# Three weight tiles through the contraction side by side at the start, and the bias table's copy moved into the pairs

## The chip, the cores and the metric

The kernel runs on one core of a Trainium2 chip. TensorE (PE) multiplies, with its weight loads shown on a row of their own (PEld); VectorE (DVE), ScalarE (ACT) and GpSimd (POOL) do the element-wise work; SyncE (SP) issues most transfers. The metric is the device time of one execution in microseconds (us); the time before is the median of three runs. One execution was also taken with the hardware profiler; all rows and stages below are of that execution, counted from its first instruction.

## The reference

One layer of a streaming encoder, 512 tokens of 1024 features, all float32. Two SwiGLU feed-forward parts (FFN 1 and FFN 2, hidden width 2816) stand around a mixer with a gated linear recurrence and a sliding-window attention. What matters here is FFN 1 and the bias of the attention:

```python
h = x + 0.5 * post1(SwiGLU_1(pre1(x)))
# swiglu(x, w1, w3, w2) = (silu(x @ w1) * (x @ w3)) @ w2
# rms_norm(x, g)        = x * rsqrt(mean(x * x) + 1e-6) * g
u = pre_mix(h)
# ... q, k, v, recurrent branch A, attention branch B with a shared relative-position bias ...
bias = band_rel_bias(rel_bias)     # (heads, 64, 192), from a (32 buckets, 16 heads) table
sc = sc + bias
h = h + post_mix(merged @ w_o)
y = h + 0.5 * post2(SwiGLU_2(pre2(h)))
```

## The kernel before, in words

Every float32 operand of a product is split in two float32r parts: hi is ACT's rounded copy, lo is DVE's difference (`split2`, L173). A product is then three matmuls, hi by hi, lo by hi, hi by lo (`mm_feat`, L185 to L187). A weight tile is 128 x 1024: one output block of 128 features by the whole contraction of 1024, which is eight blocks `k` of 128. One tile against x^T of all 512 tokens is a *unit*: 24 matmuls of 512 columns into one PSUM bank.

`order` lists the weight tiles in the order of their use. `dma_to(n)` issues loads up to the n-th on SP (L129), `split_to(n)` splits them (L140, L141), and `get` takes the next tile and keeps two splits and three loads ahead. SBUF tiles come from one pool of 38 equal slots (`NSLOT`, L1071). A new tile that takes a slot waits until the slot's last user has finished, and that wait is put on the first instruction that touches the new tile. Each engine runs its instructions in the order in which the code emits them. `later(n, fn)` defers emission by n `point()`s, one of which comes at each half unit.

The start (L546 to L601): nine matmuls on zeros (L561) run first. SP issues the table `vec`, the first w1 tile in two parts, x^T in eight row blocks of 256 KB (L554), then the next weight tiles and x. For each `k`, ACT and DVE scale the block of x^T by the norm's gain and split it into `uT` (L583, L584). Then come the units w1 0, w3 0, w1 1 (L585), one after the other over all eight blocks, then the squares of x and the inverse root mean square (`rstd_of`, L589 to L593), the unit w3 1, and a product `r` that spreads the inverse root over the partitions (L598). `Rb` is its copy, and `silu_mul` applies it to the banks.

The bias table: POOL loads a one-hot table and `rel_bias` (L625, L626). One product makes the 16 x 383 row table (L628), DVE evicts it into `erow` (L630), and POOL issues a transfer that writes it 128 times for each head into DRAM as `bias_scr`, 3064 KB (L633). The attention reads it much later (`bias_load`, L890).

FFN 1 goes on with units up to hidden block 5 (`swiglu_units`, `NC1`), then with `Pairs` (L433): hidden blocks two by two, each pair of w1 blocks a *job*, each pair of w3 blocks the next one, sixteen jobs counted from 0. A job makes seven half-size products in place of eight from sums of weight quarters and of x quarters. `prep(m, 0)` lets POOL form the sums S12 and S34 of job m (L470 to L473), `prep(m, 1)` to `prep(m, 4)` split tiles and sums. `run` (L486) emits job n: the products a11 and s1, each copied by ACT (q1 at L501, q5 at L503), the last product a22 of the job before (`last`), `prep(n+1, 1)`, s2, `prep(n+1, 2)`, a12, s4, `prep(n+1, 3)`, s3 with ACT's copy `v` (L520), `prep(n+1, 4)`, `prep(n+2, 0)` and the loads of job n+3. Before the first job four splits write further x sums into `uT` (L690 to L693).

Of the kernel before, what the change touches and what calls it, by code (L numbers as in the profile page):

```python
# [10 lines left out]
F32 = mybir.dt.float32  # L11
F32R = mybir.dt.float32r
AF = mybir.ActivationFunctionType
ALU = mybir.AluOpType

P = 128
SEQ = 512
D = 1024
KT = D // P
# [3 lines left out]
N_HEADS = 16  # L23
# [5 lines left out]
NREL = 383  # L29
# [22 lines left out]
def hybrid_layer(ctx: ExitStack, tc: tile.TileContext, a: dict, out: bass.AP):  # L52
    nc = tc.nc
    act, dve, pool, pe, sp = nc.scalar, nc.vector, nc.gpsimd, nc.tensor, nc.sync
# [8 lines left out]
    def slot(shape, dt=F32, name="s"):  # L63
        uid[0] += 1
        return sb.tile(shape, dt, tag="slot", name=f"{name}_{uid[0]}")

    def bank(name="ps"):
        uid[0] += 1
        return pp.tile([P, 512], F32, tag="ps", name=f"{name}_{uid[0]}")
# [5 lines left out]
    def f32(ap):  # L75
        return ap.bitcast(F32)
# [10 lines left out]
    uT = cp.tile([P, 2, KT, SEQ], F32R, name="uT")  # L87


    order = []  # L90
# [31 lines left out]
    st = {"dma": 0, "split": 0, "get": 0}  # L122
    raws, pairs = {}, {}

    def dma_to(n):
        while st["dma"] < min(n, len(order)):
            nm, i = order[st["dma"]]
            r = slot([P, D], name=f"raw_{nm}{i}")
            sp.dma_start(out=r, in_=a[nm][i * P : (i + 1) * P, :])  # L129
            raws[st["dma"]] = r  # L130
            st["dma"] += 1

    def split_to(n):
        while st["split"] < min(n, len(order)) and st["split"] not in paired:
            k = st["split"]
            dma_to(k + 1)
            r = raws.pop(k)
            hi = slot([P, D], F32R, name="whi")
            lo = slot([P, D], F32R, name="wlo")
            act.activation(hi, r, AF.Copy)  # L140
            dve.tensor_tensor(out=lo, in0=r, in1=f32(hi), op=ALU.subtract)  # L141
            pairs[k] = (hi, lo)
            st["split"] += 1
# [29 lines left out]
    def split2(hi, lo, src):  # L173

        act.activation(hi, src, AF.Copy)  # L175
        dve.tensor_tensor(out=lo, in0=src, in1=f32(hi), op=ALU.subtract)  # L176
# [14 lines left out]
    def unit(nm, i, **kw):  # L191
        w = get(nm, i)
        ps = bank("f")
        mm_feat(ps, w, **kw)
        return ps
# [225 lines left out]
    def mm_s(wa, x, ps, more=False):  # L421

        wh, wl = wa
        for k in range(4):
            s = slice(k * P, (k + 1) * P)
            xh, xl = x(0, k), x(1, k)
            first = k == 0 and not more
            pe.matmul(ps, wh[:, s], xh, start=first, stop=False, skip_group_check=True)  # L428
            pe.matmul(ps, wl[:, s], xh, start=False, stop=False, skip_group_check=True)  # L429
            pe.matmul(ps, wh[:, s], xl, start=False, stop=k == 3, skip_group_check=True)  # L430
        point()

    class Pairs:  # L433
# [49 lines left out]
                W["a22"] = t[:, 0, :], t[:, 1, :]  # L483
                del W["r"], W["s"]

        def run(self, tail):  # L486
            X = self.X
            assert st["get"] == st["split"] == self.k0, (st, self.k0)
            st["get"] = st["split"] = self.k0 + 2 * len(self.jobs)
            last = lambda: None  # L490
            for n, (nm, f) in enumerate(self.jobs):
                W = self.w.pop(n)
                first = nm == self.na
                tmp = slot([P, 4, 256], name="ct")
                q1, q5, u, v = (tmp[:, i, :] for i in range(4))
                c = slot([P, 2, SEQ], name="cc")
                if first:
                    self.c1[f] = c
                bu, bx, bc = (bank("c")[:, :256] for _ in range(3))
                mm_s(W["a11"], X["b11"], bu)  # L500
                act.activation(q1, bu, AF.Copy)  # L501
                mm_s(W["s1"], X["t1"], bx)
                act.activation(q5, bx, AF.Copy)  # L503
                last()
                self.prep(n + 1, 1)
                mm_s(W["s2"], X["t2"], bu, True)
                del W["s1"], W["s2"]
                act.activation(u, bu, AF.Copy)
                if n == len(self.jobs) - 1:
                    tail()  # L510
                self.prep(n + 1, 2)
                mm_s(W["a12"], X["b21"], bc)
                del W["a11"], W["a12"]
                dve.tensor_tensor(out=c[:, 0, :256], in0=bc, in1=q1, op=ALU.add)
                mm_s(W["s4"], X["b22"], bx, True)
                dve.tensor_tensor(out=c[:, 0, 256:], in0=bx, in1=u, op=ALU.add)
                self.prep(n + 1, 3)
                mm_s(W["s3"], X["t3"], bu, True)
                del W["s3"], W["s4"]
                act.activation(v, bu, AF.Copy)  # L520
                dve.tensor_tensor(out=c[:, 1, 256:], in0=v, in1=q5, op=ALU.add)
                if first:
                    act.activation(c[:, 0, :], c[:, 0, :], AF.Silu)
                    act.activation(c[:, 1, 256:], c[:, 1, 256:], AF.Silu)
                else:
                    c1 = self.c1[f]
                    dve.tensor_tensor(out=c1[:, 0, :], in0=c1[:, 0, :], in1=c[:, 0, :], op=ALU.mult)
                    dve.tensor_tensor(out=c1[:, 1, 256:], in0=c1[:, 1, 256:], in1=c[:, 1, 256:], op=ALU.mult)
                self.prep(n + 1, 4)
                self.prep(n + 2, 0)  # L530
                self.raws(n + 3)

                def last(W=W, bu=bu, c=c, f=f, first=first):
                    mm_s(W.pop("a22"), X["t4"], bu, True)
                    if first:
                        act.activation(c[:, 1, :256], bu, AF.Silu)
                    else:
                        c1 = self.c1.pop(f)
                        dve.tensor_tensor(out=c1[:, 1, :256], in0=bu, in1=c1[:, 1, :256], op=ALU.mult)
                        self.hid.f += [c1[:, 0, :], c1[:, 1, :]]  # L540

            last()

    raw = slot([P, D], name="raw_first")  # L546
    hi, lo = slot([P, D], F32R, name="whi"), slot([P, D], F32R, name="wlo")
    pairs[0] = (hi, lo)
    st["dma"] = st["split"] = 1
    parts = (slice(0, 2 * P), slice(2 * P, D))  # L550
    xts = [slot([P, 2, SEQ], name="xt") for _ in range(KT // 2)]

    def load_x(k):
        sp.dma_start(out=xts[k // 2][:, k % 2, :], in_=a["xT"][k * P : (k + 1) * P, :])  # L554


    warm = slot([P, 512], F32R, name="warm")
# [2 lines left out]
    for _ in range(WARM):  # L560
        pe.matmul(psw, warm[:, :P], warm, start=True, stop=True)  # L561

    sp.dma_start(out=vec, in_=a["vec"])
    sp.dma_start(out=raw[:, parts[0]], in_=a["w1a"][0:P, parts[0]])
    load_x(0)
    load_x(1)
    sp.dma_start(out=raw[:, parts[1]], in_=a["w1a"][0:P, parts[1]])
    for k in range(2, KT):
        load_x(k)
    dma_to(4)  # L570
    for t in range(NT):
        sp.dma_start(out=h_all[:, t, :], in_=a["x"][t * P : (t + 1) * P, :])
    make_identity(nc, ident)
    ones = slot([P, P], name="ones")
    pool.memset(ones, 1.0)
    for k in range(KT):
        if k in (0, 2):
            c = parts[k // 2]
            act.activation(hi[:, c], raw[:, c], AF.Copy)
            dve.tensor_tensor(out=lo[:, c], in0=raw[:, c], in1=f32(hi[:, c]), op=ALU.subtract)  # L580
        g = vec[:, V_G1 + k : V_G1 + k + 1]
        xk = xts[k // 2][:, k % 2, :]
        act.activation(uT[:, 0, k, :], xk, AF.Copy, scale=g)  # L583
        dve.scalar_tensor_tensor(out=uT[:, 1, k, :], in0=xk, scalar=g, in1=f32(uT[:, 0, k, :]), op0=ALU.mult, op1=ALU.subtract)  # L584
    ps = [unit("w1a", 0), unit("w3a", 0), unit("w1a", 1)]  # L585
    s4 = small(NT, "s4")
    for t in range(NT):
        junk = slot([P, D], name="junk")
# [32 lines left out]
        dve.tensor_scalar(out=cneg, in0=z[3], scalar1=-8.0, scalar2=None, op0=ALU.mult)  # L621


    oh = slot([N_BUCKETS, NREL + 1 + N_HEADS], name="oh")
    pool.dma_start(out=oh[:, : NREL + 1], in_=a["onehot"])  # L625
    pool.dma_start(out=oh[:, NREL + 1 :], in_=a["rel_bias"])  # L626
    pse = bank("e")
    pe.matmul(pse[:N_HEADS, : NREL + 1], oh[:, NREL + 1 :], oh[:, : NREL + 1], start=True, stop=True)  # L628
    erow = slot([N_HEADS, NREL + 1], name="erow")
    dve.tensor_copy(erow, pse[:N_HEADS, : NREL + 1])  # L630
    scr = tc.dram_tile([N_HEADS, P, NREL], F32, name="bias_scr")
    ev = erow[:, :NREL]
    pool.dma_start(out=scr, in_=bass.AP(tensor=ev.tensor, offset=ev.offset, ap=[ev.ap[0], [0, P], ev.ap[1]]))  # L633

    def swiglu_units(na, nb, f0, f1, hid, R=None):
        for f in range(f0, f1):
# [46 lines left out]
    pairs_a = Pairs("w1a", "w3a", NC1, X1, hid)  # L683
# [16 lines left out]
        hid.to(2)  # L700
        split_to(st["split"] + 1)

    pairs_a.run(w2_ahead)
    X1 = pairs_a = None
    later(10, softplus)
    bs = tok_gemm("w2a", hid, FT, RF, "ffn1_post_g", 0.5, "mix_pre_g", [("xr", i) for i in range(4)], hid.to)
    hid = None
# [101 lines left out]
    for i in range(8):  # L809
        ps = unit("wg", i)  # L810
# [320 lines left out]
```

## Time and profile before

| | |
|---|---|
| median of three runs | 1161.41 us (1159.35 to 1165.38) |
| the profiled execution | 1161.51 us, span 1159.7 us |
| mean granted TensorE clock | 0.994 |
| PE busy / DVE / ACT / POOL | 98% / 67% / 50% / 32% of the span |
| transfers | 120.73 MB, mean 104 GB/s |

A row of the timeline gives start, duration, engine, line, operation, what it writes from what, and in brackets the idle time of the engine before it with what ended that. A row of the chain of waits gives start, length and what the chain passed through. A row of a stage gives its length, then busy time and number of instructions for PE, PEld, DVE, ACT and POOL, then the granted clock, the share of the transfer engines and GB/s. A matmul's busy time overlaps the next one's; the distance of two starts is its real cost.

### The profile page before, as it was taken

Reading aid. Unit: us, or ns where it says so; the run is one execution under the profiler, and the core shown is the slowest. Engines: PE = TensorE matmul, PEld = TensorE weight load, DVE = VectorE, ACT = ScalarE, POOL = GpSimd, SP = SyncE. Lnnn points to the kernel's source line nnn. Section 1 sums busy time; section 2 is a strip of 40 time slices with the busy share of each in tenths; the row PEclk is TensorE's granted clock in tenths of the full one; section 3 lists DMA queues with packets and bytes.
Section 4 is the critical chain, followed back from the end, with each engine's and each line's share of the span. In section 5 each row is a group of like instructions: output and inputs, shape, how many; then the busy total and the mean of one; then the engine's idle time right before and its main releaser. Section 6 shows DMA issues by size and latency. Waiting matters only on the chain.

```text
span 1159.7 us, 17087 instructions
## 1 busy us (share of the span) xinstructions
PE 1139.1 (98%) x6691; PEld 1011.0 (87%) x6691; DVE 776.8 (67%) x1179; ACT 578.9 (50%) x1023; POOL 365.6 (32%) x271
## 2 busy tenths in 40 slices
PE   8989999999999999999999999999999999999997
PEld 6879999988888888878888788888899999998886
DVE  4997788876437742697667863667868688885313
ACT  6345555564324446864646565355645555564211
POOL 0246777600001001101556550000646667700000
PEclk9999999999999999999999999999999999999999
DMA  9663332254314122224132224342133223254101
GB/s 363 104 135 92 110 110 92 84 207 163 109 37 128 55 62 66 74 73 156 63 91 73 73 73 127 109 146 73 37 110 109 83 100 110 92 176 170 54 19 54
DMA packets 34496, 120.73 MB, mean 104 GB/s; under 512 B 4144, under 2 KB 4272, under 8 KB 34416
## 3 DMA queue, kind: packets, MB, share of 16 engines
q1 hardware_dynamic: 31968, 111.22, 28.3%
q0 software_dynamic: 2448, 8.43, 3.8%
q8 instruction: 52, 0.85, 0.3%
q14 instruction: 28, 0.23, 0.1%
HBM read 114.40 MB, written 5.23 MB: 103 GB/s over the span
## 4 chain that ended last, share of the span: by engine, by line
PE 81%; DVE 8%; ACT 5%; DMA 4%; issue 1%; POOL 1%; SPq 0%; DVEq 0%; POOLq 0%; ACTq 0%
PE c L428 10%; PE c L429 10%; PE c L430 10%; PE f L187 8%; PE f L186 8%; PE f L185 8%; PE acc L205 8%; PE acc L203 8%; PE acc L204 8%; DMA bias_scr<-erow 3%; DVE wlo L141 1%; PE pt L945 1%; POOL P L929 1%; ACT whi L140 1%; DVE ig_e L771 1%
## 5 line engine op out<-in xcount | busy, mean ns | idle before, releaser
L185 PE MATMUL f<-uT,whi 128*128 128x512 f32 (+1 forms) x560 | 206.3, 368 | 1.4 <-ACT uT L583 0.9
L186 PE MATMUL f<-uT,wlo 128*128 128x512 f32 (+1 forms) x560 | 205.1, 366 | 2.4 <-DVE wlo L141 2.4
L187 PE MATMUL f<-uT,whi 128*128 128x512 f32 (+1 forms) x560 | 204.9, 366 | 0.7 <-DVE uT L283 0.4
L203 PE MATMUL acc<-whi,hT 128*128 128x512 f32 x352 | 137.1, 390 | 0.0
L204 PE MATMUL acc<-wlo,hT 128*128 128x512 f32 x352 | 137.0, 389 | 0.0
L205 PE MATMUL acc<-whi,hT 128*128 128x512 f32 x352 | 136.9, 389 | 0.0
L185 PEld LDWEIGHTS f<-uT,whi 128*128 128x128 f32 x560 | 105.9, 189 | 20.5 <-ACT uT L583 2.3
L186 PEld LDWEIGHTS f<-uT,wlo 128*128 128x128 f32 x560 | 105.9, 189 | 20.1 <-DVE wlo L141 3.5
L187 PEld LDWEIGHTS f<-uT,whi 128*128 128x128 f32 x560 | 105.7, 189 | 19.1 <-DVE uT L584 1.3
L428 PE MATMUL c<-Xh,whi 128*128 128x256 f32 x408 | 116.2, 285 | 3.1 <-ACT ct L501 3.1
L176 DVE TENSOR_TENSOR wlo<-S,whi 128x1024 fp32r<-128x1024 f32 x68 | 110.8, 1630 | 8.5 <-ACT whi L175 6.6
L428 PE MATMUL c<-uT,whi 128*128 128x256 f32 x408 | 116.1, 285 | 0.0
L429 PE MATMUL c<-uT,wlo 128*128 128x256 f32 x408 | 116.1, 284 | 0.0
L429 PE MATMUL c<-Xh,wlo 128*128 128x256 f32 x408 | 116.0, 284 | 0.0
L430 PE MATMUL c<-uT,whi 128*128 128x256 f32 x408 | 116.0, 284 | 0.0
L430 PE MATMUL c<-Xl,whi 128*128 128x256 f32 x408 | 116.0, 284 | 0.0
L428 PEld LDWEIGHTS c<-Xh,whi 128*128 128x128 f32 x408 | 78.8, 193 | 3.4 <-ACT ct L501 3.3
L929 POOL TENSOR_SCALAR P<-P,d 128x256 f32<-128x256 f32 (+1 forms) x64 | 63.7, 1009 | 52.4 <-DVE d L927 41.3
L429 PEld LDWEIGHTS c<-uT,wlo 128*128 128x128 f32 x408 | 79.0, 194 | 0.0
L428 PEld LDWEIGHTS c<-uT,whi 128*128 128x128 f32 x408 | 79.0, 194 | 0.0
L430 PEld LDWEIGHTS c<-uT,whi 128*128 128x128 f32 x408 | 79.0, 194 | 0.0
L429 PEld LDWEIGHTS c<-Xh,wlo 128*128 128x128 f32 x408 | 78.9, 193 | 0.0
(304 smaller groups left out, 2662.5 us busy)
## 6 DMA issues: line engine op xcount, KB each, us to landing
raw_w3a<-in_w3a_dram SPq DMA_DIRECT2D x22, 512.0 KB, 4.3
raw_w2a<-in_w2a_dram SPq DMA_DIRECT2D x22, 512.0 KB, 4.2
raw_w1b<-in_w1b_dram SPq DMA_DIRECT2D x22, 512.0 KB, 4.1
raw_w3b<-in_w3b_dram SPq DMA_DIRECT2D x22, 512.0 KB, 4.2
raw_w2b<-in_w2b_dram SPq DMA_DIRECT2D x22, 512.0 KB, 4.3
raw_w1a<-in_w1a_dram SPq DMA_DIRECT2D x21, 512.0 KB, 4.3
raw_wg<-in_wg_dram SPq DMA_DIRECT2D x16, 512.0 KB, 3.5
raw_xr<-in_xr_dram SPq DMA_DIRECT2D x8, 512.0 KB, 3.7
```

The lines of the kernel that those rows point to most:

```text
L140: act.activation(hi, r, AF.Copy)
L176: dve.tensor_tensor(out=lo, in0=src, in1=f32(hi), op=ALU.subtract)
L185: pe.matmul(ps[:, c0:c1], wh[:, s], h_, start=k == 0, stop=False)
L186: pe.matmul(ps[:, c0:c1], wl[:, s], h_, start=False, stop=False)
L187: pe.matmul(ps[:, c0:c1], wh[:, s], l_, start=False, stop=k == KT - 1)
L203: pe.matmul(acc[n], x[:, 0, c], wh[:, s], start=first, stop=False)
L204: pe.matmul(acc[n], x[:, 0, c], wl[:, s], start=False, stop=False)
L205: pe.matmul(acc[n], x[:, 1, c], wh[:, s], start=False, stop=last)
L428: pe.matmul(ps, wh[:, s], xh, start=first, stop=False, skip_group_check=True)
L429: pe.matmul(ps, wl[:, s], xh, start=False, stop=False, skip_group_check=True)
L430: pe.matmul(ps, wh[:, s], xl, start=False, stop=k == 3, skip_group_check=True)
L929: pool.tensor_scalar(out=pt[:, x, b0:256], in0=pt[:, x, b0:256], scalar1=d[:, x : x + 1], scalar2=None, op0=ALU.mult)
```

## The change

Three things are changed in the source.

At the start the first three weight tiles are loaded in quarters of 128 x 256 (`load_w`), interleaved with the row blocks of x^T; the first row block is issued by ACT. For each block `k` TensorE does the three matmuls of each of the three tiles into three banks, then goes to the next block. The quarters are split one by one (`split_first`). The fourth tile is split after the loop, ahead of the squares of x.

The bias product, its eviction and the copy to DRAM become a function `spread_bias`; the eviction moves from DVE to ACT.

`Pairs.run` takes hooks; `spread_bias` is called in job 3 of FFN 1, after its first product and the copy q1.

```diff
-        def run(self, tail):
+        def run(self, tail, hooks={}):
...
+                at = lambda i: [f() for f in hooks.get((n, i), ())]
                 mm_s(W["a11"], X["b11"], bu)
                 act.activation(q1, bu, AF.Copy)
+                at(1)
                 mm_s(W["s1"], X["t1"], bx)
...
+    NS = 3
+    raw3 = [slot([P, D], name="raw_first") for _ in range(NS)]
+    pair3 = [(slot([P, D], F32R, name="whi"), slot([P, D], F32R, name="wlo")) for _ in range(NS)]
+    st["dma"] = st["split"] = st["get"] = NS
...
+    def load_w(u, kp):
+        nm, i = order[u]
+        c = slice(kp * 2 * P, (kp + 1) * 2 * P)
+        sp.dma_start(out=raw3[u][:, c], in_=a[nm][i * P : (i + 1) * P, c])
...
+    load_x(0, act)
     sp.dma_start(out=vec, in_=a["vec"])
-    sp.dma_start(out=raw[:, parts[0]], in_=a["w1a"][0:P, parts[0]])
-    load_x(0)
-    load_x(1)
-    sp.dma_start(out=raw[:, parts[1]], in_=a["w1a"][0:P, parts[1]])
-    for k in range(2, KT):
-        load_x(k)
-    dma_to(4)
+    for kp in range(KT // 2):
+        load_w(0, kp)
+        if kp:
+            load_x(2 * kp)
+        load_w(1, kp)
+        load_w(2, kp)
+        load_x(2 * kp + 1)
+    dma_to(NS + 1)
...
+    def split_first(u, kp):
+        c = slice(kp * 2 * P, (kp + 1) * 2 * P)
+        hi, lo = pair3[u]
+        split2(hi[:, c], lo[:, c], raw3[u][:, c])
+
     for k in range(KT):
-        if k in (0, 2):
-            c = parts[k // 2]
-            act.activation(hi[:, c], raw[:, c], AF.Copy)
-            dve.tensor_tensor(out=lo[:, c], in0=raw[:, c], in1=f32(hi[:, c]), op=ALU.subtract)
+        if k % 2 == 0:
+            split_first(0, k // 2)
         g = vec[:, V_G1 + k : V_G1 + k + 1]
...
+        if k % 2 == 0:
+            split_first(1, k // 2)
+            split_first(2, k // 2)
+        s_ = slice(k * P, (k + 1) * P)
+        for (hi, lo), p_ in zip(pair3, ps):
+            pe.matmul(p_, hi[:, s_], uT[:, 0, k, :], start=k == 0, stop=False)
+            pe.matmul(p_, lo[:, s_], uT[:, 0, k, :], start=False, stop=False)
+            pe.matmul(p_, hi[:, s_], uT[:, 1, k, :], start=False, stop=k == KT - 1)
+    del raw3, pair3, hi, lo
+    split_to(NS + 1)
-    ps = [unit("w1a", 0), unit("w3a", 0), unit("w1a", 1)]
...
-    pse = bank("e")
-    pe.matmul(pse[:N_HEADS, : NREL + 1], oh[:, NREL + 1 :], oh[:, : NREL + 1], start=True, stop=True)
-    erow = slot([N_HEADS, NREL + 1], name="erow")
-    dve.tensor_copy(erow, pse[:N_HEADS, : NREL + 1])
-    scr = tc.dram_tile([N_HEADS, P, NREL], F32, name="bias_scr")
-    ev = erow[:, :NREL]
-    pool.dma_start(out=scr, in_=bass.AP(tensor=ev.tensor, offset=ev.offset, ap=[ev.ap[0], [0, P], ev.ap[1]]))
+    def spread_bias():
+        pse = bank("e")
+        pe.matmul(pse[:N_HEADS, : NREL + 1], oh[:, NREL + 1 :], oh[:, : NREL + 1], start=True, stop=True)
+        erow = slot([N_HEADS, NREL + 1], name="erow")
+        act.activation(erow, pse[:N_HEADS, : NREL + 1], AF.Copy)
+        ev = erow[:, :NREL]
+        pool.dma_start(out=scr, in_=bass.AP(tensor=ev.tensor, offset=ev.offset, ap=[ev.ap[0], [0, P], ev.ap[1]]))
...
-    pairs_a.run(w2_ahead)
-    X1 = pairs_a = None
+    pairs_a.run(w2_ahead, {(3, 1): [spread_bias]})
+    X1 = pairs_a = oh = None
```

More of the change, by code (lines that the diff above doesn't have):

```diff
@@ L499, in run @@
                 bu, bx, bc = (bank("c")[:, :256] for _ in range(3))
+                at = lambda i: [f() for f in hooks.get((n, i), ())]
                 mm_s(W["a11"], X["b11"], bu)
                 act.activation(q1, bu, AF.Copy)
+                at(1)
                 mm_s(W["s1"], X["t1"], bx)
                 act.activation(q5, bx, AF.Copy)
+                at(2)
                 last()
@@ L508, in run @@
                 act.activation(u, bu, AF.Copy)
+                at(3)
                 if n == len(self.jobs) - 1:
@@ L542, in run, with load_x @@
             last()
[L546 to L550, printed above, removed]
-    xts = [slot([P, 2, SEQ], name="xt") for _ in range(KT // 2)]
-    def load_x(k):
-        sp.dma_start(out=xts[k // 2][:, k % 2, :], in_=a["xT"][k * P : (k + 1) * P, :])
+    NS = 3
+    raw3 = [slot([P, D], name="raw_first") for _ in range(NS)]
+    pair3 = [(slot([P, D], F32R, name="whi"), slot([P, D], F32R, name="wlo")) for _ in range(NS)]
+    st["dma"] = st["split"] = st["get"] = NS
+    xts = [slot([P, 2, SEQ], name="xt") for _ in range(KT // 2)]
+    def load_x(k, q=sp):
+        q.dma_start(out=xts[k // 2][:, k % 2, :], in_=a["xT"][k * P : (k + 1) * P, :])
+    def load_w(u, kp):
+        nm, i = order[u]
+        c = slice(kp * 2 * P, (kp + 1) * 2 * P)
+        sp.dma_start(out=raw3[u][:, c], in_=a[nm][i * P : (i + 1) * P, c])
     warm = slot([P, 512], F32R, name="warm")
@@ L575, in hybrid_layer @@
     pool.memset(ones, 1.0)
+    ps = [bank("f") for _ in range(NS)]
+    def split_first(u, kp):
+        c = slice(kp * 2 * P, (kp + 1) * 2 * P)
+        hi, lo = pair3[u]
+        split2(hi[:, c], lo[:, c], raw3[u][:, c])
     for k in range(KT):
-        if k in (0, 2):
-            c = parts[k // 2]
-            act.activation(hi[:, c], raw[:, c], AF.Copy)
-            dve.tensor_tensor(out=lo[:, c], in0=raw[:, c], in1=f32(hi[:, c]), op=ALU.subtract)
+        if k % 2 == 0:
+            split_first(0, k // 2)
         g = vec[:, V_G1 + k : V_G1 + k + 1]
@@ L621, in softplus @@
         dve.tensor_scalar(out=cneg, in0=z[3], scalar1=-8.0, scalar2=None, op0=ALU.mult)
+    scr = tc.dram_tile([N_HEADS, P, NREL], F32, name="bias_scr")
     oh = slot([N_BUCKETS, NREL + 1 + N_HEADS], name="oh")
```

## The prediction

> **What bounds the kernel now.** I read the page first (busy time, then the chain that ended last), then busy time by stage, then the timeline of the two places that the change touches.
>
> ```profile
> span 1159.7 us, 17087 instructions
> PE 1139.1 (98%) x6691; PEld 1011.0 (87%) x6691; DVE 776.8 (67%) x1179; ACT 578.9 (50%) x1023; POOL 365.6 (32%) x271
> ...
> 0.00:5.80 5.80, 4.21 (x9) 2.81 (x9) 0.92 (x3) 2.42 (x3) 2.04 (x9) 1.00 0.61 186
> 5.80:10.60 4.80, 3.78 (x9) 1.89 (x10) 3.45 (x5) 3.55 (x6) 0.00 (x0) 1.00 1.01 370
> 10.60:15.30 4.70, 3.97 (x18) 2.81 (x17) 4.28 (x7) 3.89 (x5) 0.00 (x0) 1.00 1.03 420
> 15.30:32.00 16.70, 16.70 (x76) 13.90 (x77) 6.62 (x14) 8.73 (x13) 0.00 (x0) 1.00 0.85 346
> ```
>
> TensorE is the bound: busy 98% of the span, so a microsecond counts only where TensorE stands still, or where work is put on it. (The stage rows give length, then busy time and count for PE, weight load, DVE, ACT, POOL, then granted clock, DMA share, GB/s.) It stands still at the start: 27 matmuls in the 9.5 us from 5.8 to 15.3, while the DMA engines are full. The profiled execution took 1161.51 us, its span plus 1.8; the median of the runs is 1161.41, so the sum is made against 1161.5 and holds for the median.
>
> **The start.** The first four tile products are 96 matmuls.
>
> ```profile
> 5.81 0.80 PE L185 MATMUL f<-uT,whi 128*128 128x512 f32 x1 [0.15 <-ACT uT L583]
> 12.89 1.06 ACT L140 ACTIVATE whi<-raw_w3a 128x1024 fp32r<-128x1024 f32 x1 [0.52 <-DMA raw_w3a<-in_w3a_dram]
> 15.26 0.51 PE L186 MATMUL f<-uT,wlo 128*128 128x512 f32 x1 [0.73 <-DVE wlo L141]
> 25.72 1.05 ACT L589 ACTIVATE junk<-h_all 128x1024 f32<-128x1024 f32 x1
> 29.48 0.87 DVE L593 TENSOR_SCALAR dgs<-ident,r 128x128 f32<-128x128 f32 x4
> 31.44 0.23 PE f L187
> 31.66 0.91 PE r L598 x8
> 33.23 0.50 PE L185 MATMUL f<-uT,whi 128*128 128x512 f32 x1
> 37.77 0.54 DVE L630 COPY erow<-e 16x384 f32<-16x384 f32 x1
> ```
>
> Back to back a matmul takes 0.23 us (the row of 31.44, from the chain; 0.227 over 72 of them, 15.26 to 31.66). Without waits 96 need 21.8 us and would end at 27.6; they end at 31.66, so 4.0 us is the most the start can give. In the new order x^T's row block k feeds nine matmuls (three tiles, three products each), 2.04 us, in place of three, 0.68. To load up to the last block: 1.57 MB of w, 2.10 of x^T and the small tables. By the GB/s of the stage rows 1.1 MB is in by 5.8, 2.9 by 10.6, the rest by about 13; were the 1 KB rows of the quarter tiles to move at half the rate, 3.7 us later, about 16.5. TensorE needs the last block only after 63 matmuls, at 5.8 + 14.3 = 20.1. So the arrival is covered on both bounds from the second block on. On SP 20 issues at 0.42 to 0.5 us each (next fence) end near 10.5; the fourth product's tile and x follow it and come about 3 us later than now.
>
> ```profile
> 1.18 0.42 SPq L564 DMA_DIRECT2D raw_first<-in_w1a_dram  x1
> 3.06 3.01 SPq L554 DMA_DIRECT2D xt<-in_xT_dram  x6
> ```
>
> The fourth tile then lands near 16 and is split by 18.5, needed at 22.3: covered. The rstd chain runs 25.72 to 30.35 now from the last square on (rows above); its squares no longer stand behind a weight tile's split on ACT, so it ends by 26 to 29, against need at 27.9. The twelve quarter splits (0.42 us each on ACT and DVE) lie beside 4.1 us of matmuls per pair of blocks. I take 0.5 us lost while the first three quarters trickle in: the four products end at 28.15, **gain 3.5** (bounds 2.5 and 4.0). The bias product leaves this place, too: 33.23 - 32.57 = 0.66, so the next tile starts 4.15 earlier. It comes back in the pairs: **+0.66**. Its eviction, 0.54 us of DVE, becomes an ACT copy of about as much, beside ACT's idle time there.
>
> **The gap at 80.** The old copy's only visible wait on compute is DVE's, and it leads to a gap of TensorE:
>
> ```profile
> 72.35 1.23 DVE L176 TENSOR_TENSOR wlo<-S,whi 128x1024 fp32r<-128x1024 f32 x1 [1.68 <-DMA bias_scr<-erow]
> 74.06 1.30 POOL L470 TENSOR_TENSOR S<-raw_w3a 128x512 f32<-128x512 f32 x1 [11.42 <-DMA raw_w3a<-in_w3a_dram]
> 54.73 2.31 DVE L141 TENSOR_TENSOR wlo<-raw_w3a,whi 128x1024 fp32r<-128x1024 f32 x1
> 83.04 0.58 PE L428 MATMUL c<-Xh,whi 128*128 128x256 f32 x1 [3.13 <-ACT ct L501]
> 79.90:83.00 3.10, 0.01 (x1) 0.00 (x0) 3.10 (x4) 3.10 (x5) 0.12 (x1) 0.82 0.64 244
> 83.00:88.70 5.70, 5.66 (x26) 5.66 (x27) 5.70 (x4) 3.48 (x5) 5.10 (x3) 0.50 0.53 157
> 88.70:92.00 3.30, 3.30 (x30) 3.30 (x29) 3.30 (x4) 0.42 (x2) 3.10 (x2) 1.00 0.13 51
> ```
>
> The gap costs 3.1 us, and then 26 matmuls run at the halved clock: 5.7 us against some 3.1 at 0.12 each (last row: 30 in 3.3, the ones at the edges cut), so 2.6 more. With the copy gone, DVE's 1.68 goes, and its 0.5 us eviction. What is late next is POOL against DVE: the 11.42 us wait of POOL is for a tile that crawled beside the copy; it now comes about 4 us after its issue, so POOL's four S sums run beside the same DVE splits, and a split that takes 1.23 alone takes 2.31 beside POOL (rows 1 and 3). One or two splits slowed by 1.1 eat the 1.68; and four ACT writes to uT must in any case follow the last tile product. I keep this gap as it is: **0**, with -5.0 (most of gap and slow clock gone) and +0.5 as ends.
>
> **The copy in its new place.** In the changed program it is issued in job 3 of `Pairs.run` (jobs counted from 0), after the first product. What it costs, by the old place:
>
> ```profile
> 38.60 1.03 POOL L633 DMA_DIRECT2D bias_scr<-erow  x1 [35.90 <-DVE erow L630]
> bias_scr<-erow POOLq DMA_DIRECT2D x1, 3064.0 KB, 33.7
> 39.00:40.00 1.00, 1.00 (x6) 0.81 (x5) 1.00 (x3) 0.97 (x2) 0.64 (x1) 1.00 0.03 8
> raw_w3a<-in_w3a_dram SPq DMA_DIRECT2D x2, 512.0 KB, 14.4
> raw_w1a<-in_w1a_dram SPq DMA_DIRECT2D x1, 512.0 KB, 14.6
> ...
> raw_w1a<-in_w1a_dram SPq DMA_DIRECT2D x4, 512.0 KB, 4.0
> 117.37 0.81 SPq L129 DMA_DIRECT2D raw_w1a<-in_w1a_dram  x2
> 137.65 1.56 SPq L129 DMA_DIRECT2D raw_w1a<-in_w1a_dram  x2
> 41.00:44.00 3.00, 3.00 (x15) 2.47 (x14) 3.00 (x7) 0.00 (x0) 0.00 (x0) 1.00 0.97 103
> ```
>
> 33.7 us, and not because of others: from 41 to 44 it moves 103 GB/s by itself at a full DMA share. Until it lands, `erow`'s slot can't be reused. In the built order of the changed program the first to wait for that is POOL's L472 sum into S34 of job 6 (`prep(6, 0)`, emitted at the end of job 4), seven POOL instructions behind the copy; L473 is queued behind it. ACT's split of that S34 stands in job 5, and behind it in ACT's queue the copy `v` of job 5, which TensorE needs before job 5's last product (a22), the third in job 6. The same places now:
>
> ```profile
> 113.97 0.36 ACT L501 ACTIVATE ct<-c 128x256 f32<-128x256 f32 x1
> 127.83 2.16 POOL L472 TENSOR_TENSOR S<-raw_w1a,S 128x512 f32<-128x512 f32 x1
> 137.94 2.00 ACT L175 ACTIVATE whi<-S 128x1024 fp32r<-128x1024 f32 x2
> 141.98 0.38 ACT L520 ACTIVATE ct<-c 128x256 f32<-128x256 f32 x1 [2.04 <-PE c L430]
> 144.66 0.28 PE L428 MATMUL c<-uT,w 128*128 128x256 f32 x1
> ```
>
> On this clock: q1 of job 3 at 113.97, the evicted row behind it, copy issued at 114.8, landed at 114.8 + 33.7 + 1.3 (more weight tiles beside it: the issues from 117 to 138, six tiles, are due where the old place had three) = 149.8. L472 can start 22 us late; L472 and L473 at 1.3 each without DVE beside them: 152.5; split 1.0 and `v` 0.4: the a22 product starts at 153.9, not at 144.66 + 0.66 = 145.3. **Loss 8.6**, and a gap this long halves the clock as at 80: **+2.6** (1.2 to 3.4). Bounds of the 8.6: the copy by itself, 3.14 MB at 103 GB/s and 1.4 before its first byte (nothing moves until 40), 31.9, gives 5.5; each further weight tile 1.3, four of them, 12.4. Weight tiles loaded meanwhile take 14 us in place of 4.0 (the row behind the dots, of 112 to 152 us), which job 6's rows (S12 used at 137.94) just bear, or the stall hides it.
>
> [...]
>
> **Sum**: 1161.5 - 4.15 + 0.66 + 0 + 8.6 + 2.6 = **1169.2 us**, slower by 0.66%. Own range: all gains high and the stall low 1159 (1161.5 - 4.66 - 5.0 + 0.66 + 5.5 + 1.2), the other way round 1175. About 0.5%, 5.8 us, is what a measurement of this kernel can tell from no change.
>
> **Rivals.** (1) The copy is hidden: it lands within about 26 us of its issue (145.3 - 4.1 - 114.8), or ACT isn't held. Then only the start counts: 1161.5 - 4.15 + 0.66 = 1158.0, and 1153 if the gap at 80 shrinks as well. For it: DMA share is low in this stage; against it: 103 GB/s alone. [...] 17%, half of it below 1155.6. (2) The start doesn't move: the quarters arrive so late that TensorE waits as now. Sum without 3.5: 1172.7. Against it: the 7 us between arrival and need. 6%. (3) The stall is met twice: the weight tiles held beside the copy (14.4 us each, and SP's queue behind them) make job 7 wait, too, by another 5 to 8: 1175 to 1177. For it: SP's and POOL's queues are in order; against it: POOL needs 4 x 2.2 us of a job's 10. 10%.
>
> **Chances.** Forecast 67%. Its range 1159 to 1175 crosses 1167.2 at about its lower third, so 21 of it are within 0.5%, 46 above; with half of (1), 8, within, 9 faster, and (2) and (3) above: faster 0.09, same 0.29, slower 0.62. Range with 8 in 10: from 1157 (the upper half of rival 1) to 1176.
>
> **What would show it.** Right: the r product starts near 28; POOL's L472 sum for job 6 begins with a wait of 10 to 20 us on the copy; one gap of TensorE of 6 to 9 us in job 6 ended by ACT's `ct` copy, with a half-clock stretch behind it. Wrong: no wait on the copy in POOL's rows, or the copy's landing time far from 34 to 37; a first block of products that ends after 30; no gap at 80.

## The result, and the profile after

| | median | range |
|---|---|---|
| before | 1161.57 us | 1159.35 to 1165.38 |
| after | 1172.39 us | 1172.34 to 1175.91 |

The ratio is 1.0090 with a 95% interval of 1.0072 to 1.0108: slower by 0.9%. The forecast was 1169.2, in a range of 1157 to 1176.

The profiled execution of the changed kernel is the slowest of the four: 1175.91 us, a span of 1174.1. Up to 524 us from its start its products run 11.4 us later than before, which fits the median; 3 us more come in the attention, where its stretches of halved clock lie elsewhere and are longer than in the execution of before (mean granted clock 0.62 from 629 to 633.5 us and 0.53 from 667 to 674.2, against 0.57 from 655 to 659 before). So the account below ends at 524 us, and is set against the median.

The stage rows of the changed kernel, to be read like those of before: length, busy time and count for PE, weight load, DVE, ACT and POOL, granted clock, DMA share, GB/s. The last two rows are the stall in the pairs and what follows it.

```profile
0.00:5.80 5.80, 4.35 (x11) 3.12 (x11) 1.43 (x3) 2.62 (x4) 2.05 (x9) 1.00 0.59 173
5.80:10.60 4.80, 4.69 (x18) 3.07 (x18) 3.71 (x9) 3.88 (x9) 0.00 (x0) 1.00 1.05 355
10.60:15.30 4.70, 4.70 (x22) 3.87 (x22) 3.83 (x9) 3.69 (x9) 0.00 (x0) 1.00 1.04 339
136.00:155.20 19.20, 10.16 (x58) 9.39 (x57) 6.69 (x7) 5.73 (x9) 10.46 (x7) 0.73 0.71 181
155.20:168.00 12.80, 10.96 (x87) 10.35 (x87) 11.72 (x11) 5.03 (x11) 9.45 (x6) 1.00 0.27 83
```

From 5.8 to 15.3 us TensorE now issues 40 matmuls where it issued 27, with the DMA engines full in both (share 1.05 and 1.04 in its two rows, 1.01 and 1.03 before). From 136 to 155 it is busy for 10.2 of 19.2 us, at a mean clock of 0.73. Before, it was busy throughout this stretch, at the full clock:

```profile
136.00:155.20 19.20, 19.20 (x162) 19.20 (x161) 16.41 (x16) 9.94 (x17) 15.87 (x8) 1.00 0.32 111
```

The timeline of TensorE at the start and at the gap near 80 us:

```profile
28.10 1.05 PE L623 MATMUL r<-dgs,ones 128*128 128x128 f32 x8
28.91 0.48 PE L185 MATMUL f<-uT,whi 128*128 128x512 f32 x1
79.36 0.39 PE L428 MATMUL c<-Xh,whi 128*128 128x256 f32 x1 [3.40 <-ACT ct L502]
```

The `r` product starts 3.56 us earlier, and the tile behind it 4.32 (28.91 against 33.23). The gap near 80 is still there, 3.40 us in place of 3.13.

Then POOL, ACT and TensorE around the copy, in this order:

```profile
111.47 1.03 POOL L660 DMA_DIRECT2D bias_scr<-erow  x1 [2.19 <-ACT ct L505]
144.43 1.26 POOL L470 TENSOR_TENSOR S<-raw_w1a 128x512 f32<-128x512 f32 x1 [23.89 <-DMA raw_w1a<-in_w1a_dram]
147.11 1.27 POOL L472 TENSOR_TENSOR S<-raw_w1a,S 128x512 f32<-128x512 f32 x1
137.48 1.06 ACT L175 ACTIVATE whi<-raw_w1a 128x1024 fp32r<-128x1024 f32 x1 [4.62 <-DMA raw_w1a<-in_w1a_dram]
147.06 1.06 ACT L175 ACTIVATE whi<-S 128x1024 fp32r<-128x1024 f32 x1 [8.25 <-POOL S L471]
150.62 1.06 ACT L175 ACTIVATE whi<-S 128x1024 fp32r<-128x1024 f32 x1 [2.50 <-POOL S L473]
138.86 0.38 PE L428 MATMUL c<-uT,whi 128*128 128x256 f32 x1 [2.11 <-ACT ct L511]
148.17 0.58 PE L428 MATMUL c<-Xh,whi 128*128 128x256 f32 x1 [6.17 <-ACT whi L175]
152.02 0.56 PE L428 MATMUL c<-uT,w 128*128 128x256 f32 x1
```

Read from the bottom: TensorE stands 6.17 us for a split by ACT, ACT stands 8.25 us for a sum by POOL, and POOL has stood 23.89 us for a weight tile, not for the slot of `erow`. The last row is the a22 product of job 5, at 144.66 before: 7.36 us late. The transfers issued in this stretch (kind, count, KB each, median us from issue to landing) and the stretch of halved clock:

```profile
bias_scr<-erow POOLq DMA_DIRECT2D x1, 3064.0 KB, 34.0
raw_w1a<-in_w1a_dram SPq DMA_DIRECT2D x4, 512.0 KB, 19.6
raw_w3a<-in_w3a_dram SPq DMA_DIRECT2D x2, 512.0 KB, 23.0
144.90:155.20 10.30, 6.27 (x27) 5.90 (x28) 5.46 (x6) 4.40 (x7) 9.99 (x7) 0.50 0.48 174
```

Weight tiles that took 4 us take about 20. The second tile of job 6, issued 3.5 us behind the copy, landed 29.3 us after its issue and released POOL; the copy itself landed at 145.4.

The balance, each step as the shift of the same product between the two profiles: -4.32 at the start, -0.35 more by job 0 (the gap near 80 is followed by less halved clock: a mean of 0.64 from 79.3 to 84 us and 1.00 behind it, against 0.50 from 83 to 88.7 before), +0.93 for the bias product in job 3, then +11.10, +3.03 and +1.05 in jobs 5 to 8, together 15.2. That makes +11.44 from job 7 on, unchanged to 524 us, and 1161.5 + 11.4 = 1172.9, against a median of 1172.4.

### The profile page after: what moved, and what is told of

Read it like the earlier page. It is cut to its first block, busy times and chain, and to the rows that moved or that the text cites. A ratio compares the mean times of both kernels' runs of the same rounds, so it can differ in the third digit from the quotient of the medians.

```text
span 1174.1 us, 17123 instructions
## 1 busy us (share of the span) xinstructions
PE 1144.1 (97%) x6691; PEld 1014.7 (86%) x6691; DVE 779.1 (66%) x1186; ACT 580.3 (49%) x1032; POOL 367.2 (31%) x271
## 4 chain that ended last, share of the span: by engine, by line
PE 75%; DVE 11%; ACT 5%; DMA 3%; issue 3%; POOL 2%; SPq 0%; DVEq 0%; POOLq 0%; ACTq 0%
PE c L428 8%; PE c L429 8%; PE c L430 8%; PE f L187 8%; PE f L185 8%; PE f L186 8%; PE acc L203 8%; PE acc L204 8%; PE acc L205 8%; DMA raw_w1a<-in_w1a_dram 2%; DVE wlo L141 2%; DVE wlo L176 1%; PE pt L972 1%; ACT whi L140 1%; DVE P L941 1%
## 5 line engine op out<-in xcount | busy, mean ns | idle before, releaser
L186 PE MATMUL f<-uT,wlo 128*128 128x512 f32 (+1 forms) x536 | 195.8, 365 | 1.6 <-DVE wlo L141 1.6
L185 PE MATMUL f<-uT,whi 128*128 128x512 f32 (+1 forms) x536 | 196.7, 367 | 0.5 <-ACT uT L282 0.5
L187 PE MATMUL f<-uT,whi 128*128 128x512 f32 (+1 forms) x536 | 195.6, 365 | 0.4 <-DVE uT L283 0.4
L186 PEld LDWEIGHTS f<-uT,wlo 128*128 128x128 f32 x536 | 101.4, 189 | 18.6 <-DVE wlo L141 2.9
L187 PEld LDWEIGHTS f<-uT,whi 128*128 128x128 f32 x536 | 101.3, 189 | 17.0 <-DVE uT L283 0.9
L185 PEld LDWEIGHTS f<-uT,whi 128*128 128x128 f32 x536 | 101.4, 189 | 16.7 <-ACT uT L282 1.0
L428 PEld LDWEIGHTS c<-uT,whi 128*128 128x128 f32 x408 | 78.8, 193 | 2.3 <-ACT ct L511 2.3
L430 PEld LDWEIGHTS c<-Xl,whi 128*128 128x128 f32 x408 | 79.1, 194 | 0.0
```

Source lines behind the costliest of these rows:

```text
L185: pe.matmul(ps[:, c0:c1], wh[:, s], h_, start=k == 0, stop=False)
L186: pe.matmul(ps[:, c0:c1], wl[:, s], h_, start=False, stop=False)
L187: pe.matmul(ps[:, c0:c1], wh[:, s], l_, start=False, stop=k == KT - 1)
```

## The experiments

Two theories of the stall. **A**, the prediction's: POOL's sum into S34 waits for the slot of `erow`, which the copy holds. **B**, from the profile after: the weight tiles of job 6 stand behind the copy in the DMA engines. A third question is why the copy is slow, a fourth whether start and move add up. The median of before beside these runs was 1162.0 to 1162.4 us.

| kernel | median | ratio to before, 95% interval |
|---|---|---|
| start alone | 1158.43 us | 0.9966 (0.9955 to 0.9978) |
| move alone | 1176.90 us | 1.0120 (1.0105 to 1.0135) |
| row in its own tile | 1174.93 us | 1.0106 (1.0090 to 1.0121) |
| 128-partition source, job 3 | 1161.93 us | 1.0001 (0.9985 to 1.0016) |
| 128-partition source, old place | 1162.12 us | 1.0006 (0.9991 to 1.0020) |
| copy on ACT's queue | 1180.72 us | 1.0171 (1.0151 to 1.0192) |
| 24 KB in place of 3 MB | 1160.11 us | 0.9985 (0.9972 to 0.9997) |
| eight pieces, uT moved | 1162.04 us | 0.9998 (0.9986 to 1.0010) |
| eight pieces, uT in place | 1158.38 us | 0.9956 (0.9938 to 0.9974) |
| two pieces | 1164.38 us | 1.0015 (1.0002 to 1.0029) |

**The start alone.** The changed kernel with the lines of the bias table as they were before, and no hook:

```diff
-    pairs_a.run(w2_ahead, {(3, 1): [spread_bias]})
+    pairs_a.run(w2_ahead)
```

> The new order of the first three products, with the bias product, its row and its copy left in their old place before the fourth product's end. All theories that make the start and the copy independent: the r product starts near 28.1, the gap near 80 stays about 3.3 us long, no stall in job 6, time 1161.5 - 4.3 + 0.7 (the bias product stays) - 0.7 = 1157 us (1156 to 1158.5). If the copy's move was also needed to keep the early weight tiles flowing (the copy is issued about 4 us sooner here and meets the same tiles), some of the 4.3 is given back near 75 and the time is 1160 to 1162.

1158.43 us, 3.7 below the median of before beside it. The products of FFN 1 stand 4.19 us early from job 0 to the end. The row of its gap near 80, with the old copy in flight until 69:

```profile
79.84 0.43 PE L428 MATMUL c<-Xh,whi 128*128 128x256 f32 x1 [3.22 <-ACT ct L502]
```

3.22 us here, 3.40 with the copy gone from this place: taking the copy away does not shorten this gap. What sets it wasn't followed further.

**The move alone.** The kernel before with `spread_bias` and the hook, and its old start.

> The start as before, the bias copy moved to job 3. If the stall belongs to the move alone: 1161.5 - 0.7 (product gone from the start) + 0.9 (product in the pairs) + 15.2 (gaps and halved clock of job 6 as in the changed kernel) = 1176.9 us (1174 to 1179), copy 34 us from issue to landing, two weight tiles of job 6 at 24 to 29 us. Rival, the stall needs the earlier start (which brings the weight tiles' issues into other positions against the copy): 1162 to 1168.

1176.90 us, as the sum of the parts gives. The copy took 33.8 us, and POOL waited again for a tile:

```profile
148.55 1.26 POOL L470 TENSOR_TENSOR S<-raw_w1a 128x512 f32<-128x512 f32 x1 [23.55 <-DMA raw_w1a<-in_w1a_dram]
```

Start and move are independent, and the whole loss belongs to the move.

**The row in a tile of its own**, so that no slot is held by the copy:

```diff
-    cp.tile([P, 232], F32, name="gap")
-    sm.tile([P, 256], F32, name="gap2", bufs=1)
+    erow_own = cp.tile([P, NREL + 1], F32, name="erow_own")
+    sm.tile([P, 104], F32, name="gap2", bufs=1)
...
-        erow = slot([N_HEADS, NREL + 1], name="erow")
+        erow = erow_own[:N_HEADS, :]
+        act.activation(slot([N_HEADS, 8], name="spare"), pse[:N_HEADS, :8], AF.Copy)
```

> The changed kernel with the 16 x 384 row that the copy reads in a tile of its own, so that no later tile waits for the copy to finish; a small write takes its turn in the slots. Theory A (the prediction's: POOL's sum into S34 waits for the slot of the row): the stall goes, 1157 to 1160 us, POOL's L472 of job 6 starts with no wait. Theory B (the weight tiles of job 6 are held 24 to 29 us in the DMA engines beside the copy): POOL's L470 waits 24 us for raw_w1a as before, time unchanged at 1172 us (1171 to 1174).

1174.93 us. Theory A falls. The two sums of job 6 and the copy:

```profile
142.75 1.26 POOL L470 TENSOR_TENSOR S<-raw_w1a 128x512 f32<-128x512 f32 x1 [23.08 <-DMA raw_w1a<-in_w1a_dram]
145.43 1.27 POOL L472 TENSOR_TENSOR S<-raw_w1a,S 128x512 f32<-128x512 f32 x1
bias_scr<-erow_own POOLq DMA_DIRECT2D x1, 3064.0 KB, 35.7
```

The copy was issued at 110.59 and landed at 146.3; L472 now starts before that, so the slot's wait is gone, and the stall is nearly as long: by the shift of the products 14.5 us, against 15.2. The time is 1 to 4 us above what B gave (1171 to 1174); where that comes from, the runs with pieces show.

**A source of 128 partitions.** The table's columns are spread eight times by ACT, so that the product makes 128 rows, and the copy reads all partitions:

```diff
-        pe.matmul(pse[:N_HEADS, : NREL + 1], oh[:, NREL + 1 :], oh[:, : NREL + 1], start=True, stop=True)
+        pe.matmul(pse[:, : NREL + 1], ohw, oh[:, : NREL + 1], start=True, stop=True)
...
-        pool.dma_start(out=scr, in_=bass.AP(tensor=ev.tensor, offset=ev.offset, ap=[ev.ap[0], [0, P], ev.ap[1]]))
+        pool.dma_start(out=scr, in_=bass.AP(tensor=ev.tensor, offset=ev.offset, ap=[ev.ap[0], [0, P // 8], ev.ap[1]]))
```

> The changed kernel with the product made for 128 rows (each head eight times) so that the copy to DRAM reads 128 partitions in place of 16, the same 3.1 MB to the same addresses from the same place in job 3. If the copy is slow because it reads only 16 partitions: it lands 9 to 15 us after its issue, the weight tiles beside it take 6 to 12 us, no wait of POOL or TensorE over 2 us in job 6, time 1172.4 - 15.2 + 0 to 1 = 1157 to 1159 us. If it is slow because of its queue or because of the writes to DRAM: it takes 30 to 36 us again and the time stays at 1172 us.

In between. The stretch of the copy, with POOL's first sum of job 6:

```profile
bias_scr<-erow POOLq DMA_DIRECT2D x1, 3064.0 KB, 18.7
raw_w1a<-in_w1a_dram SPq DMA_DIRECT2D x4, 512.0 KB, 8.5
130.08 1.29 POOL L470 TENSOR_TENSOR S<-raw_w1a 128x512 f32<-128x512 f32 x1 [8.47 <-DVE cc L525]
```

The same bytes to the same addresses in 18.7 us in place of 34.0: the 16 partitions were what made it slow. (The wait is put down to DVE; the tile it reads landed at 129.93, 0.15 us ahead.) Of the 15.2 us of stall 2.05 are left, in short waits of under 1 us. Another 1 us is lost at the start (3.70 early at job 0, against 4.67); the one thing added there is ACT's spread of the columns.

**The same in the old place**, with the new start.

> The new start with the bias copy in its old place, but reading 128 partitions in place of 16. The copy of 16 partitions there costs nothing that TensorE shows (the new start alone: 1158.4 us, no gap before 75 us but the one that stands without a copy, too). Theory: hidden work stays hidden, so a copy of 19 us in place of 34 gains nothing: 1157 to 1160 us. Rival: the gap near 80 us comes from the weight tiles held beside the copy (POOL's wait for raw_w3a) and goes or shrinks with a copy that is over by 54 us: 1153 to 1156 us.

1162.12 us, and this doesn't answer its question. The copy landed after 15.4 us, but a new wait came first:

```profile
34.01 1.64 PE L658 MATMUL e<-oh 32*128 32x384 f32 x2 [4.81 <-ACT oh L656]
```

TensorE waited 4.81 us for ACT's spread of the columns. The gap near 80 was 1.16 us in this run and ended 2.7 us later than before; what shrank it is open.

**The copy on ACT's queue**, from the 16 partitions:

```diff
-        pool.dma_start(out=scr, in_=bass
+        act.dma_start(out=scr, in_=bass
```

> The changed kernel with the same copy from 16 partitions issued on ACT's queue in place of POOL's. If the 16 partitions that it reads set its rate: 30 to 36 us from issue to landing again, the weight tiles of job 6 held over 20 us again, 1170 to 1176 us. If POOL's queue sets it: it lands within 20 us and the time falls to 1158 to 1163 us.

```profile
bias_scr<-erow ACTq DMA_DIRECT2D x1, 3064.0 KB, 33.7
145.12 1.06 ACT L175 ACTIVATE whi<-raw_w3a 128x1024 fp32r<-128x1024 f32 x1 [23.10 <-DMA bias_scr<-erow]
146.50 0.58 PE L428 MATMUL c<-uT,whi 128*128 128x256 f32 x1 [19.14 <-ACT ct L511]
```

33.7 us again: not the queue. The time missed, 1180.72 us against 1170 to 1176. Here one of ACT's splits waits 23.1 us for the copy itself, and TensorE 19.1 behind it; the products fall back by 20.6 us there. Why this split waits for the copy was not traced, so the run settles the rate and not the price of the queue.

**24 KB in place of 3 MB**, with the later reads of the bias set to it; this kernel leaves out the shift of one column per row.

> Prices the copy in its new place: the changed kernel with product, row and issue in job 3 as they are, but 24.5 KB written in place of 3.1 MB; the bias blocks are then read with the same number of bytes but without the shift of one column per row (that part of the computation is left out). If the stall is the copy's alone: job 6 keeps its pace, the shift is about -3.7 us from job 2 to the end of FFN 1, and the time is 1161.5 - 3.7 = 1157.8 (1156.5 to 1159.5). If the product and the row put into TensorE's and ACT's order cause part of it: 1160 to 1166 us.

1160.11 us, 0.6 above the range for a stall that is the copy's alone. FFN 1 agrees with that theory: it is 3.96 us early from job 3's second product to its end, no wait of TensorE over 0.75 us is left in the pairs behind the gap near 80, and the weight tiles take 4 us again. Its profiled execution then fell back by 2 us in small steps between 615 and 864 us, in the attention; its executions lie between 1157.6 and 1162.9. In FFN 1 the product and ACT's eviction cost 0.94, and the stall of 15.2 is gone with the copy.

**Eight pieces.** The row in its own tile, the product in job 3, and 16 of the 128 rows written in each of the jobs 3 to 10:

```diff
+    def spread_piece(i):
+        ev = erow_own[:N_HEADS, :NREL]
+        pool.dma_start(out=scr[:, 16 * i : 16 * i + 16, :], in_=bass.AP(tensor=ev.tensor, offset=ev.offset, ap=[ev.ap[0], [0, 16], ev.ap[1]]))
...
-    pairs_a.run(w2_ahead, {(3, 1): [spread_bias]})
+    pairs_a.run(w2_ahead, {(3 + i, 1): [spread_bias] * (i == 0) + [lambda i=i: spread_piece(i)] for i in range(8)})
```

> The changed kernel with the row in a tile of its own (as in the run with that tile alone, 1174.9 us) and the copy of 16 partitions cut into eight of 392 KB, issued one job apart in jobs 3 to 10: the same bytes at the same rate on the same queue, but never more than 4 us of them queued ahead of a weight tile. If the stall comes from weight tiles that stand behind the whole copy in the DMA engines: each tile takes at most 12 us, no gap of TensorE over 1 us in jobs 4 to 12, and 1158 to 1161 us. [...]

The stall was gone (FFN 1 ends 4.37 us early), but the time was 1162.04. From 404 to 475 us the kernel fell behind by some 0.03 us per us, without a gap, and again, more slowly, from 690 on; so had the run with the row's own tile. Both have `erow_own` ahead of `uT`, 608 bytes longer than the tile that it replaces. So the row went to free space behind the other tiles:

```diff
-    erow_own = cp.tile([P, NREL + 1], F32, name="erow_own")
-    sm.tile([P, 104], F32, name="gap2", bufs=1)
+    cp.tile([P, 232], F32, name="gap")
+    sm.tile([P, 256], F32, name="gap2", bufs=1)
+    op = ctx.enter_context(tc.tile_pool(name="op", bufs=1))
+    erow_own = op.tile([P, NREL + 1], F32, name="erow_own")
```

> The eight pieces again, with the row in free space behind the other tiles, so that uT and h_all keep their addresses. In the run of the pieces before this one (and in the run with the row's own tile) uT lay 608 bytes further and the matmuls that read it drifted late by some 0.03 us per us of such products, 4 us in all, with no gap to show for it. If the address was the cause: the mean of the first-projection matmuls between 405 and 475 us is back at 389 ns from 394 to 398, the shift at the end of FFN 1 is -4.4 us and stays there, and the time is 1157 to 1159 us. If the pieces cost later: 1161 to 1163 us again.

1158.38 us. The group of one of the three products of a unit, hi by lo, from 405 to 475 us (busy us, mean ns of one, idle before), with uT moved:

```profile
L187 PE MATMUL f<-uT,whi 128*128 128x512 f32 x85 | 33.8, 398 | 0.0
```

and with uT in place, where the same product stands two lines further down:

```profile
L189 PE MATMUL f<-uT,whi 128*128 128x512 f32 x87 | 33.8, 389 | 0.0
```

The two other products of a unit took 394 ns with uT moved and 389 in place.

In this last kernel the stage of the stall is full, and each piece and tile lands in about 5 us:

```profile
136.00:155.20 19.20, 19.20 (x163) 19.20 (x162) 16.36 (x17) 9.93 (x19) 14.68 (x10) 1.00 0.65 144
...
raw_w1a<-in_w1a_dram SPq DMA_DIRECT2D x4, 512.0 KB, 5.3
raw_w3a<-in_w3a_dram SPq DMA_DIRECT2D x4, 512.0 KB, 4.6
bias_scr<-erow_own POOLq DMA_DIRECT2D x5, 383.0 KB, 5.5
```

The same bytes from the same 16 partitions on the same queue, and no stall: theory B holds. What hurts is how much of the copy goes ahead of a weight tile: in pieces of 383 KB, which landed in 5.5 us, it cost nothing in this stage; the whole of 3064 KB, which landed in 34.0 us, cost 15.2.

**Two pieces** of 1.57 MB, in jobs 3 and 7.

> As the eight pieces with the row in free space, but two pieces of 1.57 MB in jobs 3 and 7, about 17 us each. If a weight tile has to stand behind all packets of the copy that are queued ahead of it, the first tile after each piece moves nothing for 7 to 14 us and lands after 15 to 20, and each piece costs 1 to 4 us of TensorE: 1160 to 1165 us. If only a copy longer than the tiles' lead of about 20 us hurts: no gap over 1 us and 1157 to 1159 us.

```profile
bias_scr<-erow_own POOLq DMA_DIRECT2D x1, 1532.0 KB, 17.3
132.26 1.29 POOL L472 TENSOR_TENSOR S<-raw_w1a 128x512 f32<-128x512 f32 x1 [12.59 <-DMA raw_w1a<-in_w1a_dram]
```

1164.38 us. (Lines stand two further down in this kernel: its L472 is L470 above.) The first tile behind the piece landed 16.5 us after its issue, just behind the piece (130.87 and 129.03), and POOL's first sum of job 6 waited 12.59 us for the second. The first piece cost 3.3 us, the second 2.3. Beside the other runs this gives a scale, by the time that job 6's second tile took to land and what the stage then lost: 6.8 us and nothing (small pieces), 13.9 and 2.1 (128 partitions), 17.3 and 3.3 (two pieces), 29.3 and 15.2 (the changed kernel).

## Why the prediction was right or wrong

The time was in its own range and the direction right, but the wait that the forecast named is not the one that cost the time.

- **The start**: right. The `r` product at 28.10, predicted 28.15; the tile behind it 4.32 early, predicted 4.15. x^T came in time, and rival 2 is out. That the 1 KB rows of the quarters might move at half the rate was an assumption for the later bound, and no run shows it: from 5.8 to 10.6 and from 10.6 to 15.3 us the engines moved 355 and 339 GB/s, against 370 and 420 before.
- **The bias product in the pairs**: predicted 0.66, its price at the start. It costs 0.93; why it costs more there was not followed.
- **The gap at 80**: predicted 0, its length kept at 3.1. It is 3.40 and brings less halved clock, in sum -0.35. With the old copy still in flight it is 3.22. That it would stay without the copy was right; that POOL beside DVE sets it was argued and not shown.
- **The length of the copy**: right, 34.0 us for 33.7 + 1.3. (The 1.3 stands there for three more tiles, while the bound gives 1.3 to each; the copy grew by 0.3.) Rival 1 (hidden) lives from a copy of under 26 us; the run with 128 partitions made it so, and came to 1161.9.
- **The failed step** is the sentence that weight tiles "take 14 us in place of 4.0", which job 6's rows "just bear, or the stall hides it". Job 6's two tiles took 23.7 and 29.3 us. The row of 14.4 was a median over two tiles, 20.9 and 7.9 us. The third tile of the old place, at 14.6, was issued at 39.47, only 0.9 us behind the copy, and 89 packets of the copy went ahead of it. Here two tiles come 2.3 and 3.5 us behind the copy, some 340 of its packets went ahead of the first (the rows stand below), and two more tiles follow 10 us later.
- **The slot**: the wait for `erow`'s slot, the step that the sum was made from, did not bind: L472 started at 147.11, 1.7 us after the copy had landed, because L470 had waited longer. Behind it the forecast's chain held: the split of that sum (150.62), the copy `v` (151.59), the a22 product (152.02). The sum still came near, because both waits end when the copy is nearly done; that is luck, and not the mechanism that was forecast. That the slot alone would have cost nearly as much is argued from these times and not shown; no run here has the slot's wait without the tiles'.
- **The size of the stall**: 8.6 + 2.6 = 11.2 predicted, 15.2 measured: 11.1 until job 5's last product, and 4.1 more in the two jobs behind it. Of the 15.2, some 3 are halved clock (an estimate: in the row of 144.90 27 matmuls are busy for 6.27 us, at 0.12 each 3.2 at the full clock) and some 12 are waits. So the halved clock was priced about right, and the waits 3.5 too low. The 4.1 are the end of the halved clock and, from 161 to 168, three waits of 0.5 to 0.8 us for DVE's splits and an ACT copy, while POOL, with the tiles of the next jobs late as well, ran its sums back to back until 164.8. That is part of rival 3, at less than its 5 to 8. The 4.0 us are the error of the forecast, up to the smaller terms.

The runs price the copy by the partitions that it reads. From 16 it moved 103 GB/s alone (before, 41 to 44 us) and landed after 34.0 us on POOL's queue and 33.7 on ACT's. From 128 it moved 259 GB/s by itself (114.8 to 121 us), 2.5 times as much, and landed after 18.7.

The packets of the changed kernel by queue (packets, MB, share of 16 engines), first from 113.7 to 129 us, where two weight tiles had been issued and then two more, then from 129 to 136:

```profile
q0 software_dynamic: 341, 1.57, 96.8%
...
q0 software_dynamic: 148, 0.68, 81.6%
q1 hardware_dynamic: 136, 0.52, 18.1%
```

For 15 us the tiles' queue moved nothing at all; then both moved, about one to one (148 packets to 136), each of the copy's packets holding an engine some four times as long as a tile's (81.6% for 148 against 18.1% for 136). The copy's packets until the first packet of a tile, now in the run with 128 partitions (114.8 to 121 us, from the tile's issue) and in the kernel before (38.6 to 44 us, from the copy's issue):

```profile
q0 software_dynamic: 346, 1.59, 103.1%
...
q0 software_dynamic: 89, 0.41, 67.5%
```

From 128 partitions as many packets went ahead, but they were over in 6.3 us. In the old place the tile was issued while POOL was still issuing the copy (38.60 to 39.63), and the tile's packets began after 4.7 us. That a tile stands behind those packets of the copy that are queued when it is issued fits these rows, and no run shows more of it; what sets their number was not tried.

## What to carry to other kernels

Before a large transfer is moved into a stage that lives on just-in-time loads, ask not only who waits for the transfer, but which loads are issued right behind it, and what lead they have; and whether they come as soon behind the transfer as in the place that a price is taken from. A tile issued 0.9 us behind the copy in the old place had 89 of its packets ahead of it, and one issued 2.3 us behind it in the new place some 340. Here tiles that landed 7 us after their issue cost nothing, and at 29 us they cost 15. A source on 16 partitions made the copy about twice as slow as one on 128 (34 us against 15 to 19); cut into pieces of 5.5 us it was harmless from 16 partitions, too. And when a tile is added for an experiment, put it where no other tile moves.

The best two versions are the new start with the copy left where it was (1158.4 us) and the new start with the copy in eight pieces (1158.4 us); their intervals overlap, and the first is the simpler.

## What the runs showed beside

- Shifting `uT` (with `h_all`) by 608 bytes made matmuls of 512 columns that read it 5 to 9 ns longer in the groups (394 to 398 against 389), and the kernel 3.7 us slower (1162.04 against 1158.38), with no idle time ahead of these groups. What it is about the address was not tried.
- A load issued 1.9 to 2.9 us behind the whole copy, on SP's queue beside POOL's, moved no packet until some 300 to 390 of the copy's packets had gone, from 16 partitions and from 128 alike: 13.4 to 15.4 us from 16, 6.3 and 6.4 from 128. Issued 0.9 us behind it, the load waited for some 90 packets, 4.7 us (before, and with the start alone). In the changed kernel both queues moved from 129 us on (148 packets to 136 up to 136 us); why not before is open.
